# RMSNorm factors moved from GpSimd to ScalarE and VectorE, one row block cut in halves, and the first gain row spread by TensorE

## The chip, the cores and the metric

The kernel runs on one core of one Trainium2 chip. The metric is the device time of one execution in microseconds (us), the median of three runs. Five engines work side by side: TensorE (PE in the profile), VectorE (DVE), ScalarE (ACT), GpSimd (POOL) and SyncE (SP), which only issues transfers here. Each engine takes its own instructions strictly in the order in which they were written; between engines, semaphores hold an instruction back until what it reads is there.

## The reference

Four residual layers over a matrix x of 512 tokens by 1024 channels, in float32. Each layer has two sublayers, a token mixer (retention, Conformer convolution, short gated convolution, retention again) and a squared-ReLU MLP with 4096 hidden channels. Each sublayer is wrapped in two norms:

```
x <- x + RMSNorm_post( f( RMSNorm_pre(x) ) )
RMSNorm(v) = v / sqrt(mean(v*v over 1024 channels) + 1e-6) * gain
```

So between two sublayers a post-norm of the sublayer's output f, a residual add and the pre-norm of the next sublayer must be done, for all 512 tokens, and nothing of the next sublayer's product can begin before some of them are through. There are seven such places, called boundaries here, in the order of time: first (retention to MLP, layer 0), second (MLP to Conformer), third (Conformer to MLP), fourth (MLP to short convolution), fifth (short convolution to MLP), sixth (MLP to retention, layer 3), seventh (retention to MLP). The head before the first sublayer has pre-norms only, the tail after the last MLP has post-norms only.

## The kernel before, in words

Tokens are four blocks b = 0 to 3 of 128 rows (the partitions); x and f are tiles of 128 x 4 x 1024. Every float32 matrix product is made of three products of a high and a low part: the high part is a rounded copy made on ACT (`hi`, `whi`, `xin[:, 0]`), the low part the difference made on DVE (`lo`, `wlo`, `xin[:, 1]`). Weights arrive by DMA as 512 KB pieces in two buffers `raw`; line 271 (ACT) and line 282 (DVE) split them (`fetch`, `settle`), and a buffer's next load is issued by SP after its `wlo`.

A boundary is the second half of `out_final`. PE works through the last output product block by block (`block(b)`); after each block DVE or ACT adds the bank to f (`evac`), ACT squares it and sums over the row (`square`, line 415), GpSimd makes the factor (mean + 1e-6)^(-1/2) in two instructions of one column (`rstd`, lines 396 to 399), DVE multiplies f by the post gain (`fold`, line 420) and adds f times the factor to x (`add`, line 428). Then ACT sums x*x (`pre_sum`), GpSimd makes the second factor, DVE writes the normed row block into `bnd` (`pre_norm`, line 434), PE turns it (`transposes`, line 445), and `place` splits the turned block into the high and low part of `xin` (ACT line 376, DVE line 377). After block 3 PE goes on with `first_four`: eight parts of the next sublayer's first products, on the tokens of blocks 0 and 1 alone. Within it, ahead of part 3, stand the transposes of block 2, and ahead of part 7 those of block 3. The low part of `place(1)` is needed by the first part's last four products (line 340).

The order of instructions on each engine is the order of these calls in the code. In the Conformer alone a planner (`Plan`) orders the work by costs; the change does not touch it. In the head, x and the gain row arrive by DMA; the gain row (4 KB) is read 128 times by a broadcasting DMA. While nothing can be multiplied yet, `warm` runs small products.

Of the kernel before, what the change touches and what calls it, by code (L numbers as in the profile page):

```python
# [8 lines left out]
F32 = mybir.dt.float32  # L9
F32R = mybir.dt.float32r  # L10
I32 = mybir.dt.int32
AF = mybir.ActivationFunctionType
# [31 lines left out]
WARM0, WARM1 = 20, 22  # L44
# [156 lines left out]
class Trunk:  # L201
# [24 lines left out]
    def tiny(self):  # L226
        return self.cp.tile([P, 1], F32, tag="tiny", bufs=16, name=self.nm("tiny"))
# [164 lines left out]
    def rstd(self, parts):  # L392
        nc = self.nc
        ms, r = self.tiny(), self.tiny()
        if len(parts) == 2:
            nc.gpsimd.tensor_scalar(ms, parts[0], parts[1], EPS, op0=ALU.add, op1=ALU.add)  # L396
        else:
            nc.gpsimd.tensor_scalar(ms, parts[0], EPS, None, op0=ALU.add)
        nc.gpsimd.tensor_tensor(r, ms, self.neg_half, op=ALU.pow)
        return r  # L400

    def begin_boundary(self, post, pre):
# [5 lines left out]
        if pre is not None:  # L408
            nc.sync.dma_start(t[:, 1, :], self.norm_g[pre[0], pre[1]:pre[1] + 1, :].broadcast_to([P, D]))
            self.xin = self.big.tile([P, 2, 8, S], F32R, tag="xin", name=self.nm("xin"))  # L410
        self.bnd = t

    def sumsq(self, src, junk):
        acc = self.tiny()
        self.nc.scalar.activation(junk, src, AF.Square, scale=1.0 / 32.0, accum_out=acc)  # L415
        return acc
# [5 lines left out]
    def post_norm(self, b):  # L422
        self.r1[b] = self.rstd(self.sums[b])
        self.fold(b)
# [5 lines left out]
    def pre_sum(self, b):  # L430
        self.r2[b] = self.rstd([self.sumsq(self.x[:, b, :], self.bnd[:, 2 + b % 2, :])])

    def pre_norm(self, b):
        self.nc.vector.scalar_tensor_tensor(self.bnd[:, 2 + b % 2, :], self.x[:, b, :], self.r2[b],  # L434
                                            self.bnd[:, 1, :], op0=ALU.mult, op1=ALU.mult)
# [67 lines left out]
    def out_final(self, slots, mode, layer_end):  # L503
# [17 lines left out]
        def square(b, dh):  # L521
            self.sums[b].append(self.sumsq(self.f[:, b, dh * 512:(dh + 1) * 512], self.tmp()))
# [26 lines left out]

        if self.next_pre is None:  # L550
            half = slice(0, 512), slice(512, D)
            for b in range(4):
# [5 lines left out]
                else:  # L558
                    for n in range(2):
# [6 lines left out]
                        self.sums[b].append(self.sumsq(f, self.tmp()[:, :256]))  # L566
                        if n == 0:
                            t = self.tiny()
                            nc.gpsimd.tensor_tensor(t, *self.sums[b], op=ALU.add)
                            self.sums[b] = [t]  # L570
# [36 lines left out]
        post(3)  # L607
# [937 lines left out]
```

## Time and profile before

| | us |
|---|---|
| median of 3 runs (2546.22 to 2547.99) | 2546.35 |
| the profiled execution's own time | 2545.85 |
| its span, first to last instruction | 2544.1 |
| busy: PE / DVE / ACT / POOL | 2516.4 / 1652.9 / 1210.3 / 218.4 |
| mean granted TensorE clock | 0.998 |

The profile is of one execution, which lies 0.50 us under the median. Time outside the span (1.75 us) is that of starting and ending. Matmuls are pipelined and their ends are modelled, so PE at 99% says that it nearly always had work, and what can be seen best is where it waited. Busy time of an engine that nobody waits for costs nothing.

### The profile page before, as it was taken

What the parts mean: (1) busy time and instruction counts of PE and PEld (TensorE: products, weight loads), DVE (VectorE), ACT (ScalarE), POOL (GpSimd) and SP (SyncE); (2) the same over time, 40 slices, a digit from 0 to 9 for tenths busy, and PEclk for the clock granted to TensorE, in tenths of its full rate; (3) what the DMA queues carried; (4) which work ended last, traced back from release to release, by engine and by line L of the source; (5) the groups of instructions that cost most, each with busy time, mean ns of one, the idle gap of its engine ahead of it and who ended that gap; (6) DMA issues with size and microseconds to landing.
All of it is one profiled execution on the core that took longest, in us unless ns stands there. A gap on an engine that the chain in (4) does not pass through costs nothing. (4 is left out here: it accounts for less than half of the span.)

```text
span 2544.1 us, 30985 instructions
## 1 busy us (share of the span) xinstructions
PE 2516.4 (99%) x12173; PEld 2124.6 (84%) x12173; DVE 1652.9 (65%) x2151; ACT 1210.3 (48%) x1829; POOL 218.4 (9%) x248
## 2 busy tenths in 40 slices
PE   9999999999999999999999999999999999999998
PEld 8888888888888788888888888888888888888887
DVE  7665346897758977677464476784646534677773
ACT  3543444555436656544332365444344334455542
POOL 1000002000027820000010100000100000200000
PEclk9999999999999999999999999999999999999999
DMA  4323234224423532332332333314322223421331
GB/s 160 104 88 109 78 127 172 97 102 170 153 92 108 188 128 100 124 133 91 116 100 99 108 116 133 133 52 155 128 79 80 95 90 106 162 106 67 133 124 67
DMA packets 85026, 290.94 MB, mean 114 GB/s; under 512 B 9488, under 2 KB 11280, under 8 KB 84880
## 3 DMA queue, kind: packets, MB, share of 16 engines
q1 hardware_dynamic: 84880, 288.96, 32.7%
q8 instruction: 95, 1.56, 0.2%
q14 instruction: 51, 0.42, 0.0%
HBM read 265.79 MB, written 21.50 MB: 113 GB/s over the span
## 5 line engine op out<-in xcount | busy, mean ns | idle before, releaser
L337 PE MATMUL bank<-xin,whi 128*128 128x512 f32 (+1 forms) x2112 | 753.3, 365 | 2.3 <-ACT xin L376 2.3
L338 PE MATMUL bank<-xin,wlo 128*128 128x512 f32 (+1 forms) x2112 | 750.3, 364 | 0.0
L282 DVE TENSOR_TENSOR wlo<-raw,whi 128x1024 fp32r<-128x1024 f32 x340 | 416.8, 1234 | 426.5 <-ACT whi L271 425.2
L271 ACT ACTIVATE whi<-raw 128x1024 fp32r<-128x1024 f32 x340 | 354.8, 1053 | 428.9 <-DMA raw<-wall 214.7
L340 PE MATMUL bank<-xin,whi 128*128 128x512 f32 (+1 forms) x2112 | 473.8, 364 | 3.2 <-DVE xin L377 3.2
L337 PEld LDWEIGHTS bank<-xin,whi 128*128 128x128 f32 x2112 | 398.9, 189 | 65.0 <-ACT xin L376 2.9
L338 PEld LDWEIGHTS bank<-xin,wlo 128*128 128x128 f32 x2112 | 399.0, 189 | 62.2
L340 PEld LDWEIGHTS bank<-xin,whi 128*128 128x128 f32 x2112 | 369.3, 189 | 67.1 <-DVE xin L377 4.8
L266 ACT ACTIVATE whi<-blk 128x1024 fp32r<-128x1024 f32 x168 | 174.5, 1053 | 123.1 <-DVE blk L303 117.0
L280 DVE TENSOR_TENSOR wlo<-blk,whi 128x1024 fp32r<-128x1024 f32 x168 | 204.8, 1221 | 19.9 <-ACT whi L266 18.7
L396 POOL TENSOR_SCALAR tiny<-tiny,tiny 128x1 f32<-128x1 f32 x32 | 52.3, 1635 | 1484.7 <-ACT tmp L415 1483.5
L1200 ACT ACTIVATE tmp<-bank 128x512 f32<-128x512 f32 x128 | 75.2, 588 | 133.0 <-PE bank L340 133.0
L1287 DVE TENSOR_TENSOR f<-f,bank 128x512 f32<-128x512 f32 x168 | 108.4, 681 | 0.0
L1067 POOL TENSOR_TENSOR pbuf<-pbuf 128x512 f32<-128x512 f32 x69 | 100.5, 1473 | 16.0 <-ACT pbuf L1064 12.7
L327 PE MATMUL bank<-whi,hid 128*128 128x512 f32 (+1 forms) x264 | 101.5, 385 | 0.0
L329 PE MATMUL bank<-whi,hid 128*128 128x512 f32 (+1 forms) x264 | 101.0, 383 | 0.0
L328 PE MATMUL bank<-wlo,hid 128*128 128x512 f32 (+1 forms) x264 | 101.0, 383 | 0.0
L327 PE MATMUL bank<-whi,y 128*128 128x512 f32 x256 | 99.9, 390 | 0.0
L327 PE MATMUL bank<-whi,xin 128*128 128x512 f32 x256 | 99.6, 389 | 0.0
L329 PE MATMUL bank<-whi,y 128*128 128x512 f32 x256 | 99.6, 389 | 0.0
L328 PE MATMUL bank<-wlo,y 128*128 128x512 f32 x256 | 99.6, 389 | 0.0
L328 PE MATMUL bank<-wlo,xin 128*128 128x512 f32 x256 | 99.6, 389 | 0.0
(224 smaller groups left out, 4135.6 us busy)
## 6 DMA issues: line engine op xcount, KB each, us to landing
raw<-wall SPq DMA_DIRECT2D x340, 512.0 KB, 3.3
blk<-wall SPq DMA_DIRECT2D x96, 512.0 KB, 5.4
park<-x SPq DMA_DIRECT2D x20, 512.0 KB, 2.6
x<-park SPq DMA_DIRECT2D x20, 512.0 KB, 4.5
bnd<-norm_g SPq DMA_DIRECT2D x16, 512.0 KB, 6.8
phase<-tmp SPq DMA_DIRECT2D x32, 256.0 KB, 2.0
x<-x_in SPq DMA_DIRECT2D x8, 512.0 KB, 6.5
whi<-phase SPq DMA_DIRECT2D x8, 512.0 KB, 6.9
```

Of the source, the lines that this page charges most:

```text
L266: nc.scalar.activation(hi, self.form_of(c, n), AF.Copy)
L271: nc.scalar.activation(hi, self.raws[i], AF.Copy)
L280: nc.vector.tensor_sub(lo, self.form_of(c, n), hi.bitcast(F32))
L282: nc.vector.tensor_sub(lo, self.raws.pop(i), hi.bitcast(F32))
L327: nc.tensor.matmul(out, ah, bh, start=start, stop=False)
L328: nc.tensor.matmul(out, ah, bl, start=False, stop=False)
L329: nc.tensor.matmul(out, al, bh, start=False, stop=stop)
L337: self.nc.tensor.matmul(out, wh[:, c], x, start=kt == 0, stop=False)
L338: self.nc.tensor.matmul(out, wl[:, c], x, start=False, stop=False)
L340: self.nc.tensor.matmul(out, wh[:, kt * P:(kt + 1) * P], self.xin[:, 1, kt, t0:t1], start=False, stop=kt == 7)
L1067: nc.gpsimd.tensor_tensor(accs[c], accs[c], pbuf[:, slot, :], op=ALU.add)
L1287: nc.vector.tensor_add(f, f, bank)
```

## The change

Three things change. (1) `rstd`: instead of two GpSimd instructions, ACT makes a first value with its table of the reciprocal square root (`seed`), and DVE makes one Newton step on it in three instructions of one column. Where a row's sum comes in two parts, DVE first adds the first part and the 1e-6 (`more`), and the seed reads that sum. ACT thereby needs this table in the boundaries; its other tables stay as they were. (2) In a boundary, block 3 is added to x, summed and pre-normed in two halves of 512 columns. (3) In the head the first gain row is loaded once, into one partition, and spread to 128 by two products with a row of ones; the loads of x and of the first weights alternate; `warm` runs 6 and 8 products instead of 20.

```diff
-WARM0, WARM1 = 20, 22
+WARM0, WARM1 = (6, 8), 22
...
             self.nc.vector.tensor_sub(lo, val, hi.bitcast(F32))
-    def rstd(self, parts):
+    def sumsq(self, src, junk):
+        acc = self.tiny()
+        self.nc.scalar.activation(junk, src, AF.Square, scale=1.0 / 32.0, accum_out=acc)
+        return acc
+    def more(self, sums, src, junk):
         nc = self.nc
-        ms, r = self.tiny(), self.tiny()
-        if len(parts) == 2:
-            nc.gpsimd.tensor_scalar(ms, parts[0], parts[1], EPS, op0=ALU.add, op1=ALU.add)
+        acc = self.sumsq(src, junk)
+        if not sums:
+            sums.append(self.eps)
         else:
-            nc.gpsimd.tensor_scalar(ms, parts[0], EPS, None, op0=ALU.add)
-        nc.gpsimd.tensor_tensor(r, ms, self.neg_half, op=ALU.pow)
+            base = self.tiny()
+            nc.vector.tensor_scalar(base, sums[1], sums[0], None, op0=ALU.add)
+            sums[:] = [base]
+        sums.append(acc)
+    def seed(self, sums):
+        r0 = self.tiny()
+        self.nc.scalar.activation(r0, sums[1], AF.Abs_reciprocal_sqrt, bias=sums[0])
+        sums.append(r0)
+    def rstd(self, sums):
+        nc = self.nc
+        base, acc, r0 = sums
+        t, r = self.tiny(), self.tiny()
+        nc.vector.tensor_scalar(t, acc, base, r0, op0=ALU.add, op1=ALU.mult)
+        nc.vector.tensor_scalar(t, t, r0, -0.5, op0=ALU.mult, op1=ALU.mult)
+        nc.vector.tensor_scalar(r, t, 1.5, r0, op0=ALU.add, op1=ALU.mult)
         return r
     def begin_boundary(self, post, pre):
...
         if post is not None:
             nc.sync.dma_start(t[:, 0, :], self.norm_g[post[0], post[1]:post[1] + 1, :].broadcast_to([P, D]))
         if pre is not None:
-            nc.sync.dma_start(t[:, 1, :], self.norm_g[pre[0], pre[1]:pre[1] + 1, :].broadcast_to([P, D]))
+            self.gain = t[:, 1, :]
+            nc.sync.dma_start(self.gain, self.norm_g[pre[0], pre[1]:pre[1] + 1, :].broadcast_to([P, D]))
             self.xin = self.big.tile([P, 2, 8, S], F32R, tag="xin", name=self.nm("xin"))
         self.bnd = t
-    def sumsq(self, src, junk):
-        acc = self.tiny()
-        self.nc.scalar.activation(junk, src, AF.Square, scale=1.0 / 32.0, accum_out=acc)
-        return acc
     def fold(self, b, cols=slice(0, D)):
         f = self.f[:, b, cols]
         self.nc.vector.tensor_mul(f, f, self.bnd[:, 0, cols])
     def post_norm(self, b):
+        self.fold(b)
         self.r1[b] = self.rstd(self.sums[b])
-        self.fold(b)
     def add(self, b, cols=slice(0, D)):
         x = self.x[:, b, cols]
         self.nc.vector.scalar_tensor_tensor(x, self.f[:, b, cols], self.r1[b], x, op0=ALU.mult, op1=ALU.add)
-    def pre_sum(self, b):
-        self.r2[b] = self.rstd([self.sumsq(self.x[:, b, :], self.bnd[:, 2 + b % 2, :])])
-    def pre_norm(self, b):
-        self.nc.vector.scalar_tensor_tensor(self.bnd[:, 2 + b % 2, :], self.x[:, b, :], self.r2[b],
-                                            self.bnd[:, 1, :], op0=ALU.mult, op1=ALU.mult)
+    def pre_sum(self, b, parts=(slice(0, D),)):
+        self.sums2[b] = []
+        for c in parts:
+            self.more(self.sums2[b], self.x[:, b, c], self.bnd[:, 2 + b % 2, c])
+        self.seed(self.sums2[b])
+    def pre_norm(self, b, parts=(slice(0, D),)):
+        r = self.rstd(self.sums2.pop(b))
+        for c in parts:
+            self.nc.vector.scalar_tensor_tensor(self.bnd[:, 2 + b % 2, c], self.x[:, b, c], r,
+                                                self.gain[:, c], op0=ALU.mult, op1=ALU.mult)
     def transposes(self, b):
         nc = self.nc
...
-            self.sums[b].append(self.sumsq(self.f[:, b, dh * 512:(dh + 1) * 512], self.tmp()))
+            self.more(self.sums[b], self.f[:, b, dh * 512:(dh + 1) * 512], self.tmp())
+            if dh:
+                self.seed(self.sums[b])
 
...
-                        self.sums[b].append(self.sumsq(f, self.tmp()[:, :256]))
-                        if n == 0:
-                            t = self.tiny()
-                            nc.gpsimd.tensor_tensor(t, *self.sums[b], op=ALU.add)
-                            self.sums[b] = [t]
+                        self.more(self.sums[b], f, self.tmp()[:, :256])
...
-        post(3)
+        self.post_norm(3)
+        for c in half:
+            self.add(3, c)
+        if layer_end:
...
-                self.pre_sum(3)
-                self.pre_norm(3)
+                self.pre_sum(3, half)
+                self.pre_norm(3, half)
...
-            self.ln_eps = self.const(LN_EPS, "ln_eps")
+            self.ln_eps, self.eps = self.const(LN_EPS, "ln_eps"), self.const(EPS, "eps")
+            self.table(AF.Abs_reciprocal_sqrt)
-            self.r1, self.r2, self.turned = {}, {}, {}
+            self.r1, self.sums2, self.turned = {}, {}, {}
-            for b in range(2):
-                nc.sync.dma_start(self.x[:, b, :], self.x_in[b])
-            self.begin_boundary(None, (LAYERS[0], 0))
-            self.load()
-            self.load()
-            for b in range(2, 4):
+            self.begin_boundary(None, None)
+            self.xin = big.tile([P, 2, 8, S], F32R, tag="xin", name="xin0")
+            row, self.gain, one = self.bnd[0:1, 0, :], self.bnd[:, 1, :], self.tmp(P)[0:1, :]
+            nc.vector.memset(one, 1.0)
+            nc.sync.dma_start(row, self.norm_g[LAYERS[0], 0:1, :])
+            for b in range(4):
...
-                self.r2[b] = self.rstd([self.sumsq(self.x[:, b, :], self.f[:, b, :])])
+                self.sums2[b] = []
+                self.more(self.sums2[b], self.x[:, b, :], self.f[:, b, :])
+                self.seed(self.sums2[b])
...
-            self.warm(WARM0)
+            self.warm(WARM0[0])
+            for n in range(2):
+                bank, c = self.bank(), slice(512 * n, 512 * n + 512)
+                nc.tensor.matmul(bank, one, row[:, c], start=True, stop=True)
+                nc.vector.tensor_copy(self.gain[:, c], bank)
+            self.warm(WARM0[1])
```

Of 64 factors, 32 post and 32 pre, each now has three DVE instructions and one ACT instruction of one column in place of two of GpSimd; where there are two parts, one more DVE instruction stands ahead. The program has four more ACT table loads: one ahead of the first seed of the first, the third and the seventh boundary, one in the last retention.

DVE in the fourth boundary, from the post-norm of block 3 to its pre-norm, before (`wlo` is the weight split, `xin` the placing of block 2, L434 the pre-norm):

```order
L420 TENSOR_TENSOR f_8227<-f_8227,bnd_10031 128x1024
L428 SCALAR_TENSOR_TENSOR x_9768<-f_8227,tiny_10365,x_9768 128x1024
L282 TENSOR_TENSOR wlo_10376<-raw_10133,whi_10375 128x1024
L282 TENSOR_TENSOR wlo_10432<-raw_10163,whi_10431 128x1024
L377 TENSOR_TENSOR xin_10034<-bank_10421,xin_10034 128x4x128
L377 TENSOR_TENSOR xin_10034<-bank_10426,xin_10034 128x4x128
L434 SCALAR_TENSOR_TENSOR bnd_10031<-x_9768,tiny_10444,bnd_10031 128x1024
```

and now, at the same place (L406 is the sum of the first part, L420 to L422 the Newton step, L458 the pre-norm):

```order
L420 TENSOR_SCALAR tiny_10524<-tiny_10511,tiny_10513,tiny_10515 128x1
L421 TENSOR_SCALAR tiny_10524<-tiny_10524,tiny_10515 128x1
L422 TENSOR_SCALAR tiny_10525<-tiny_10524,tiny_10515 128x1
L447 SCALAR_TENSOR_TENSOR x_9899<-f_8358,tiny_10525,x_9899 128x512 x2
L282 TENSOR_TENSOR wlo_10537<-raw_10264,whi_10536 128x1024
L282 TENSOR_TENSOR wlo_10593<-raw_10294,whi_10592 128x1024
L377 TENSOR_TENSOR xin_10165<-bank_10582,xin_10165 128x4x128
L377 TENSOR_TENSOR xin_10165<-bank_10587,xin_10165 128x4x128
L406 TENSOR_SCALAR tiny_10606<-tiny_10602,eps 128x1
L420 TENSOR_SCALAR tiny_10610<-tiny_10604,tiny_10606,tiny_10608 128x1
L421 TENSOR_SCALAR tiny_10610<-tiny_10610,tiny_10608 128x1
L422 TENSOR_SCALAR tiny_10611<-tiny_10610,tiny_10608 128x1
```

Three small instructions stand ahead of the add, which is now two halves, and four ahead of the pre-norm; the first of these four makes the operand of the seed, and it stands behind the weight splits and the placing of block 2.

SP at the start of the program, before (`early` is the first weight tiles):

```order
L1387 DMA x_91<-x_in 128x1024 x2
L409 DMA bnd_95<-norm_g 128x1024
L252 DMA early<-wall 128x1024 x2
L1392 DMA x_91<-x_in 128x1024
L252 DMA early<-wall 128x1024
```

and now:

```order
L1418 DMA bnd_95<-norm_g 1x1024
L1420 DMA x_93<-x_in 128x1024
L252 DMA early<-wall 128x1024
L1420 DMA x_93<-x_in 128x1024
L252 DMA early<-wall 128x1024
```

The broadcast of the gain (128 rows) is gone, its one row stands first, and the second block of x stands behind the first weight tile.

## Rows read from the trace of the kernel before

**Rows 1.** Waits of PE in the whole span: line, whom for, us, times, longest.
```profile
PE bank L445 <- DVE bnd L434: 8.2, 8, 2.5
...
PE bank L340 <- DVE xin L377: 3.2, 8, 0.9
PE bank L337 <- ACT xin L376: 2.3, 2, 2.0
```

**Rows 2.** Timeline of DVE, fourth boundary: start, us, instruction, idle before and its releaser.
```profile
1273.15 1.28 DVE L434 SCALAR_TENSOR_TENSOR bnd<-x,tiny,bnd 128x1024 f32<-128x1024 f32 x1 [1.58 <-POOL tiny L399]
...
1275.55 1.22 DVE L420 TENSOR_TENSOR f<-f,bnd 128x1024 f32<-128x1024 f32 x1
1276.87 1.28 DVE L428 SCALAR_TENSOR_TENSOR x<-f,tiny,x 128x1024 f32<-128x1024 f32 x1
...
1279.27 0.68 DVE L515 TENSOR_TENSOR f<-f,bank 128x512 f32<-128x512 f32 x1
1280.33 1.29 DVE L434 SCALAR_TENSOR_TENSOR bnd<-x,tiny,bnd 128x1024 f32<-128x1024 f32 x1 [0.39 <-POOL tiny L399]
1281.54 1.22 DVE L420 TENSOR_TENSOR f<-f,bnd 128x1024 f32<-128x1024 f32 x1
1283.52 1.29 DVE L428 SCALAR_TENSOR_TENSOR x<-f,tiny,x 128x1024 f32<-128x1024 f32 x1 [0.76 <-POOL tiny L399]
...
1286.99 1.28 DVE L377 TENSOR_TENSOR xin<-bank,xin 128x512 fp32r<-128x512 f32 x2
1288.19 1.28 DVE L434 SCALAR_TENSOR_TENSOR bnd<-x,tiny,bnd 128x1024 f32<-128x1024 f32 x1
```

**Rows 3.** Timeline of PE, fourth boundary.
```profile
1278.81 0.74 PE L340 MATMUL bank<-xin,whi 128*128 128x256 f32 x4 [0.30 <-DVE xin L377]
...
1289.61 1.06 PE L445 MATMUL bank<-ident,bnd 128*128 128x128 f32 x8 [0.56 <-DVE bnd L434]
```

**Rows 4.** Timeline of DVE in the rotary set-up, one after another.
```profile
27.32 0.49 DVE L1306 TENSOR_SCALAR tmp<-tmp,small 128x512 f32<-128x512 f32 x1
27.84 0.43 DVE L1310 TENSOR_SCALAR tmp<-tmp 128x512 f32<-128x512 f32 x1
```

**Rows 5.** Groups of DVE: busy us, mean ns of one, idle before.
```profile
L843 DVE TENSOR_TENSOR mask<-ident 128x64 f32<-128x64 f32 x1 | 0.2, 219 | 0.0
...
L1364 DVE MEMSET neg_half<- 128x1 f32 x1 | 0.1, 59 | 0.8 <-PEq L1537 0.8
```

**Rows 6.** Instructions of line 231 on ACT: ns min/median/max, first and last start.
```profile
L231 ACT ACT_TABLE_LOAD  x2: 1283/1283/1283, 874.7 to 890.4; - x2
L231 ACT ACTIVATE tiny<-ln_eps x2: 203/204/206, 876.0 to 891.6; 128x1 f32<-128x1 f32 x2
```

**Rows 7.** Groups of ACT: busy us, mean ns, idle before.
```profile
L1114 ACT ACTIVATE tmp<-tmp,ln_eps 128x512 f32<-128x512 f32 x1 | 0.7, 722 | 1.1 <-DVE tmp L1111 1.1
...
L1117 ACT ACTIVATE tmp<-tmp 128x512 f32<-128x512 f32 x1 | 0.6, 630 | 0.0
```

**Rows 8.** Timeline of ACT, second boundary.
```profile
758.02 0.31 ACT L882 ACTIVATE shift<-ones 128x128 fp32r<-128x128 f32 x1 [4.21 <-DVE ones L881]
```

**Rows 9.** Timeline of ACT, sixth boundary.
```profile
1811.76 1.06 ACT L271 ACTIVATE whi<-raw 128x1024 fp32r<-128x1024 f32 x1 [6.95 <-DMA raw<-wall]
```

**Rows 10.** Timeline of DVE in the head.
```profile
8.67 2.48 DVE L434 SCALAR_TENSOR_TENSOR bnd<-x,tiny,bnd 128x1024 f32<-128x1024 f32 x2 [7.76 <-DMA bnd<-norm_g]
...
17.63 1.28 DVE L434 SCALAR_TENSOR_TENSOR bnd<-x,tiny,bnd 128x1024 f32<-128x1024 f32 x1 [0.46 <-POOL tiny L399]
...
21.57 1.27 DVE L434 SCALAR_TENSOR_TENSOR bnd<-x,tiny,bnd 128x1024 f32<-128x1024 f32 x1
```

**Rows 11.** Transfers from 0 to 22 us, rate in 40 equal slices.
```profile
GB/s 0 0 0 238 261 268 395 425 335 253 238 216 268 343 417 380 447 402 432 402 447 410 425 417 417 415 381 370 380 350 387 421 406 391 253 145 56 0 0 0
```

**Rows 12.** Timeline of DVE in the tail.
```profile
2539.58 1.41 DVE L428 SCALAR_TENSOR_TENSOR x<-f,tiny,x 128x512 f32<-128x512 f32 x2 [0.84 <-POOL tiny L399]
```

**Rows 13.** Windows: stretch, us, busy us of each engine, granted clock, DMA, GB/s.
```profile
1813.00:1817.00 4.00, 3.64 (x22) 3.65 (x23) 3.41 (x4) 1.74 (x3) 0.00 (x0) 0.72 0.40 131
```

More of the change, by code (lines that the diff above doesn't have):

```diff
@@ L226, in tiny @@
     def tiny(self):
-        return self.cp.tile([P, 1], F32, tag="tiny", bufs=16, name=self.nm("tiny"))
+        return self.cp.tile([P, 1], F32, tag="tiny", bufs=26, name=self.nm("tiny"))
     def table(self, func):
@@ L548, in post @@
                 layer_end(b)
+        half = slice(0, 512), slice(512, D)
         if self.next_pre is None:
-            half = slice(0, 512), slice(512, D)
             for b in range(4):
@@ L565, in out_final @@
                         nc.vector.tensor_add(f, f, bank[:, c])
-                        self.sums[b].append(self.sumsq(f, self.tmp()[:, :256]))
-                        if n == 0:
-                            t = self.tiny()
-                            nc.gpsimd.tensor_tensor(t, *self.sums[b], op=ALU.add)
-                            self.sums[b] = [t]
+                        self.more(self.sums[b], f, self.tmp()[:, :256])
+                    self.seed(self.sums[b])
                 self.r1[b] = self.rstd(self.sums[b])
@@ L606, in out_final @@
         self.pre_norm(2)
-        post(3)
+        self.post_norm(3)
+        for c in half:
+            self.add(3, c)
+        if layer_end:
+            layer_end(3)
         def start(i):
@@ L1377, in build @@
             self.angles = [dram.tile([P, S], F32, name=f"angle{n}") for n in range(2)]
-            self.neg_half = self.const(-0.5, "neg_half")
             self.half_pi = self.const(float(np.float32(math.pi / 2)), "half_pi")
-            self.ln_eps = self.const(LN_EPS, "ln_eps")
+            self.ln_eps, self.eps = self.const(LN_EPS, "ln_eps"), self.const(EPS, "eps")
+            self.table(AF.Abs_reciprocal_sqrt)
             self.ident = cp.tile([P, P], F32, name="ident")
```

## The prediction

> **What bounds the kernel now.** I read the page's busy times first: PE has work nearly throughout, so only its waits can be won, and whatever makes a wait longer is paid in full. The view of PE's waits then says where they lie: it waits for the pre-norm on VectorE ahead of transposes, for the low parts of the placed blocks on VectorE, and a little for the high parts on ScalarE [rows 1]. That is 8.2 + 3.2 + 2.3 = 13.7 us over the head and seven boundaries, the most that any better boundary could return. Third, the timelines of one ordinary boundary, the fourth: the reader is to see that VectorE works from 1273.15 to the pre-norm of block 3 at 1288.19 almost without a hole; its two holes, 0.39 and 0.76 us, end on GpSimd [rows 2]. PE waits for VectorE twice there, 0.30 us for the low part of block 1 and 0.56 us for the pre-norm of block 3 [rows 3]. So VectorE's own queue, not GpSimd's delay alone, sets the end of a boundary.
>
> **The price of the new small instructions.** None of the kinds on one column is in the trace of before, so I bound it. VectorE's two-input instruction takes 219 ns on 64 columns [rows 5] and 0.68 us on 512 [rows 2]: 1.03 ns a column, and 0.15 us left at one column. A scalar read from memory adds 0.49 - 0.43 = 0.06, and an instruction that needs the one before it starts 0.03 after its end (27.32 + 0.49 to 27.84) [rows 4]. So a step of a dependent chain is 0.24 us, and a factor's three are 0.72. From below: the one-column memset takes 59 ns [rows 5]; with the wait, 0.09 a step, 0.27 for three. From above: a second scalar in the first step and 0.02 more of waiting at each, 0.85. I take 0.72, since 64 columns is the nearest row that reads its inputs. ScalarE's one-column instruction takes 0.204 [rows 6]; a bias from memory adds 722 - 630 = 92 ns [rows 7]; the seed is 0.30, 0.33 with its wait, between 0.2 and 0.4. An independent small sum costs VectorE 0.14, since neighbours overlap.
>
> On the fixed part the Trainium skill, "VectorE: DVE Perf Modes", section "The TRN2 errata", has two statements: a table by which VectorE from SBUF to SBUF needs 58 cycles plus the columns, an estimated 61 ns at one column, and beside it that the measured fixed term is about 150 cycles. The 219 ns at 64 columns speak for the second; by the first three steps would be about 0.3, and the time the one of the first rival.
>
> **One ordinary boundary, step by step.** Up to the pre-norm of block 1 the new steps come out nearly even: a factor waited 0.39 to 1.58 us for GpSimd [rows 2], now it waits for a seed and three steps; I take the shift there as -0.15. From then on VectorE is full, and what is added counts:
> - fold of block 2 to its add: 1.32 us before (1275.55 to 1276.87); now 1.14 to the next free issue, then 0.72: 1.86, so +0.54. The placing of block 1 and PE's low products come that much later.
> - drain of block 3 to pre-norm of block 2: 1.06 before (1279.27 to 1280.33); now 0.60 + 0.14 + 0.72 = 1.46, so +0.40.
> - fold to add of block 3: 1.98 before (1281.54 to 1283.52), GpSimd ending it; now 1.86, so -0.12.
> - the add in halves: two of 0.75 hold the queue for 1.34 instead of 1.20, so +0.14.
> - the weight splits and the placing of block 2 are unchanged, but then the pre-norm of block 3 followed at once (1286.99 to 1288.19), its factor having come from GpSimd meanwhile. Now the first small sum stands behind the placing, ScalarE's seed waits for that sum, and the three steps wait for the seed: 0.24 + 0.33 + 0.72 = 1.29, all uncovered.
> - the pre-norm in halves lets the first four transposes start after 0.75 instead of 1.28; PE ends them all at 2.00 after its start instead of 2.29: -0.29.
> The sum is -0.15 + 0.54 + 0.40 - 0.12 + 0.14 + 1.29 - 0.29 = +1.8 us, some 0.4 of it at the low products and the rest at the last transposes. Queued behind the waiting steps are weight splits; they come 0.8 us later, which PE does not feel, as the pieces that it reads by then are already split. Nothing behind the boundary gives the time back, for PE has no other holes.
>
> **The other boundaries.** The first, third and seventh have the same order plus a table load ahead of the first seed. A load takes 1.28 us and the next instruction starts as it ends (874.7 to 876.0) [rows 6]. Part of it hides in the wait for block 1's product; by the same steps 0.45 stays, so 2.25 each. In the fifth ScalarE drains the banks itself, and each seed delays a drain: 1.9. In the second ScalarE cannot go on before a memset that stands on VectorE behind the adds [rows 8], so its later sums move with them; 1.5. In the sixth PE ends by waiting for ScalarE, which waits 6.95 us for a weight transfer [rows 9]; the transfer is issued on SP behind the parking of block 3, so only the shift of the adds, 0.8, is paid, and the later transposes hide in that wait. Together 1.8 + 3 x 2.25 + 1.9 + 1.5 + 0.8 = 12.75. One more table load, in the last retention, stands where ScalarE waits for products: nothing; uncovered, 1.3.
>
> On such loads the Trainium skill, "ScalarE: Activation LUTs", section "What ACT_TABLE_LOAD costs", reckons a drain of 1.38 us behind the load, 2.66 in all. The starts of line 231, 1.3 us apart, show none; by the page the sum would be up to 3 x 1.4 = 4 us more.
>
> **Head and tail.** Before, the first two pre-norms waited until 8.67 for the broadcast gain [rows 10]. That wait goes: the row is there early, and two products and two copies spread it before ScalarE has block 0's sum. But block 1 of x now stands behind a 512 KB weight tile, at 400 GB/s [rows 11] 1.3 us; with its sum, seed and three steps its pre-norm starts at about 9.8, where the second of the pair started before (8.67 + 1.24 = 9.9). The first products therefore start as they did. Behind them the factors for blocks 2 and 3, until now made beside VectorE's work, stand in it: the pre-norm of block 2 goes from 17.63 to 18.1 (the second weight split waits 0.3 for two more seeds; then three steps instead of a hole of 0.46), that of block 3 from 21.57 to 22.8, and PE meets both: +1.2. In the tail the hole of 0.84 ahead of the last adds [rows 12] is refilled by seed, three steps and a fold that stood beside GpSimd before: 0, between -0.3 and +0.3.
>
> **Sum.** 12.75 + 1.2 = 13.95. On the profiled execution's 2545.85 that gives 2559.8; it lies 0.5 under the median of the runs, so 2560.
>
> **Rivals.**
> 1. Small steps are cheap, and it gets faster. Place: every three steps in the boundaries. With 0.27 for three, VectorE reaches the add of block 2 early, PE's wait for the low part goes, and transposes begin nearly on arrival: by the steps above about -0.85 in five boundaries, -1.0 in the second, -1.6 in the sixth, nothing in the head, -6.9 in all: 2539. It decides from about 0.46 for three down, where an ordinary boundary comes out even. For it: the 59 ns row. Against: every row of VectorE that reads operands, and GpSimd's holes on VectorE add to only 1.15 us in the late stretch.
> 2. Three steps near 0.46 (0.12 + 0.03 each): boundaries +0.1 to +0.4, sixth -0.6, head +0.4: 2547, no change.
> 3. The longer waits lower TensorE's clock. After two waits in the sixth boundary the granted clock averages 0.72 from 1813 to 1817 [rows 13], part of it at 1.2 GHz, which loses 4 x 0.28 = 1.1 us. If the head (fewer warming products, more holes) and all the other boundaries go that way, 7 x 1.1 = 7.7 more: 2568. Against: the longest single wait of line 445, 2.5 us [rows 1], is followed by no such stretch.
>
> **Numbers.** Forecast 58%, with its own range of 2551 to 2565; first rival 14%, second 17%, third 11%. The range for 8 in 10 reaches to 2545 below, leaving out most of the first rival, and 2570 above. About 0.2%, 5 us, is what a measurement here can tell from no change: faster 0.14, same 0.20, slower 0.66.
>
> **What would show it.** In the changed kernel's profile: small steps of lines 420 to 422 near 0.21 us each; VectorE without GpSimd holes but as late; PE's wait for the low part about 0.8 instead of 0.3 and its wait for the last transposes about 1.9 in an ordinary boundary; the pre-norm of block 1 in the head near 9.8. Small steps of 0.1 us would make the forecast wrong at its root; a head that starts 2 us earlier, or a lower clock, would be wrong in size only.

## The result and the profile after

The changed kernel takes 2567.88 us (median, 2567.65 to 2569.79); the kernel before took 2547.17 beside it (2546.22 to 2548.65). The ratio is 1.0089 with a 95% interval of 1.0076 to 1.0101: slower by 20.7 us. The forecast was 2560 with a range of 2545 to 2570; the direction and the main mechanism came as forecast, the loss was half as large again, and the time lies outside the forecast's own range of 2551 to 2565. The profiled execution took 2567.91, its span is 2566.1 (2544.1 before), the mean granted clock 0.996 (0.998).

Where the time went is read best at one place that each boundary has: the start of the first product of `first_four`. In the two profiled executions these starts stand apart as follows (each column is what a stretch adds; the last one runs to PE's last product). The sum is that of these two executions, 22.0 us; between the medians it is 20.7.

| us | head | 1st | 2nd | 3rd | 4th | 5th | 6th | 7th | sum |
|---|---|---|---|---|---|---|---|---|---|
| after minus before | 3.03 | 3.71 | 4.08 | 2.75 | 2.48 | 3.48 | -0.09 | 2.60 | 22.04 |
| forecast | 1.2 | 2.25 | 1.5 | 2.25 | 1.8 | 1.9 | 0.8 | 2.25 | 13.95 |

The tail is as it was: from the start of PE's last product to the end of the span 7.42 before and 7.41 after.

PE's waits after (line, whom for, us, times, longest) answer to [rows 1]; line 469 is the transposes there:

```profile
PE bank L469 <- DVE bnd L458: 16.9, 10, 3.0
PE bank L340 <- DVE xin L377: 9.6, 8, 1.5
...
PE bank L337 <- ACT xin L376: 0.2, 1, 0.2
```

Both waits for VectorE have grown, 8.2 to 16.9 and 3.2 to 9.6. Of the 2.3 for ScalarE the 2.0 in the sixth boundary are gone: PE's waits for VectorE ahead of it grew there from 1.3 to 3.5, so PE comes to it later. The groups of the new small instructions on VectorE (instructions, busy us, mean ns, idle before):

```profile
L422 DVE TENSOR_SCALAR tiny<-tiny,tiny 128x1 f32<-128x1 f32 x64 | 13.7, 214 | 2.2
L421 DVE TENSOR_SCALAR tiny<-tiny,tiny 128x1 f32<-128x1 f32 x64 | 13.7, 214 | 2.3
L420 DVE TENSOR_SCALAR tiny<-tiny,tiny,tiny 128x1 f32<-128x1 f32 x39 | 10.6, 271 | 7.9 <-ACT tiny L412 7.9
L406 DVE TENSOR_SCALAR tiny<-tiny,eps 128x1 f32<-128x1 f32 x39 | 8.1, 207 | 0.0
```

They last 207 to 271 ns, about as much as the 219 ns for the 64 columns of [rows 5] and three and a half to four and a half times the memset there. VectorE's timeline of the fourth boundary answers to [rows 2]:

```profile
1278.50 0.69 DVE L539 TENSOR_TENSOR f<-f,bank 128x512 f32<-128x512 f32 x1 [0.73 <-PE bank L329]
...
1286.10 0.27 DVE L420 TENSOR_SCALAR tiny<-tiny,eps,tiny 128x1 f32<-128x1 f32 x1 [0.82 <-ACT tiny L412]
...
1286.90 1.29 DVE L458 SCALAR_TENSOR_TENSOR bnd<-x,tiny,bnd 128x1024 f32<-128x1024 f32 x1
...
1289.30 1.22 DVE L439 TENSOR_TENSOR f<-f,bnd 128x1024 f32<-128x1024 f32 x1
1290.44 0.27 DVE L420 TENSOR_SCALAR tiny<-tiny,tiny,tiny 128x1 f32<-128x1 f32 x1
1290.74 0.22 DVE L421 TENSOR_SCALAR tiny<-tiny,tiny 128x1 f32<-128x1 f32 x1
1290.99 0.21 DVE L422 TENSOR_SCALAR tiny<-tiny,tiny 128x1 f32<-128x1 f32 x1
1291.24 1.28 DVE L447 SCALAR_TENSOR_TENSOR x<-f,tiny,x 128x1024 f32<-128x1024 f32 x1
...
1293.64 0.68 DVE L539 TENSOR_TENSOR f<-f,bank 128x512 f32<-128x512 f32 x1
...
1295.16 1.28 DVE L458 SCALAR_TENSOR_TENSOR bnd<-x,tiny,bnd 128x1024 f32<-128x1024 f32 x1
1296.36 1.22 DVE L439 TENSOR_TENSOR f<-f,bnd 128x1024 f32<-128x1024 f32 x1
...
1298.30 1.41 DVE L447 SCALAR_TENSOR_TENSOR x<-f,tiny,x 128x512 f32<-128x512 f32 x2
...
1301.90 1.28 DVE L377 TENSOR_TENSOR xin<-bank,xin 128x512 fp32r<-128x512 f32 x2
1303.10 0.20 DVE L406 TENSOR_SCALAR tiny<-tiny,eps 128x1 f32<-128x1 f32 x1
1303.73 0.27 DVE L420 TENSOR_SCALAR tiny<-tiny,tiny,tiny 128x1 f32<-128x1 f32 x1 [0.42 <-ACT tiny L412]
...
1304.53 1.42 DVE L458 SCALAR_TENSOR_TENSOR bnd<-x,tiny,bnd 128x512 f32<-128x512 f32 x2
```

The three steps stand between the fold of block 2 (1289.30) and its add (1291.24), with VectorE never idle: 1290.44 to 1291.24 is 0.80. At the end a chain that nothing covers: small sum at 1303.10, seed, three steps, pre-norm at 1304.53. On PE this becomes the two waits that answer to [rows 3], 1.10 instead of 0.30 and 2.02 instead of 0.56 (the expectations below count from start to start, beyond the usual spacing of the products, and call the same two waits 1.26 and 2.18):

```profile
1293.18 0.74 PE L340 MATMUL bank<-xin,whi 128*128 128x256 f32 x4 [1.10 <-DVE xin L377]
...
1305.43 1.23 PE L469 MATMUL bank<-ident,bnd 128*128 128x128 f32 x8 [2.02 <-DVE bnd L458]
```

Behind three of these waits TensorE's clock falls to its lower level, 1.2 GHz. The view by windows (stretch, us, busy us of PE, PEld, DVE, ACT, POOL, granted clock, DMA share, GB/s), behind the first, second and fifth boundary:

```profile
431.00:434.00 3.00, 3.00 (x16) 3.00 (x16) 2.86 (x4) 1.58 (x3) 0.00 (x0) 0.50 0.47 173
773.00:778.00 5.00, 4.78 (x23) 4.81 (x24) 4.48 (x6) 2.15 (x3) 0.00 (x0) 0.50 0.40 139
...
1489.00:1492.00 3.00, 3.00 (x15) 3.00 (x15) 2.69 (x4) 2.06 (x3) 0.00 (x0) 0.50 0.35 106
```

Before, these stretches ran at 1.00. Behind the sixth boundary [rows 13], in the Conformer and in the tail the clock fell before, and it falls there after as well. The third, fourth and seventh boundary have as long a wait after (2.0) and keep the full clock.

The head, on VectorE, answers to [rows 10]:

```profile
8.01 0.69 DVE L1451 COPY bnd<-bank 128x512 f32<-128x512 f32 x1 [1.01 <-PE bank L1450]
...
9.42 1.29 DVE L458 SCALAR_TENSOR_TENSOR bnd<-x,tiny,bnd 128x1024 f32<-128x1024 f32 x1
...
11.42 1.29 DVE L458 SCALAR_TENSOR_TENSOR bnd<-x,tiny,bnd 128x1024 f32<-128x1024 f32 x1
...
19.79 1.28 DVE L458 SCALAR_TENSOR_TENSOR bnd<-x,tiny,bnd 128x1024 f32<-128x1024 f32 x1
...
24.52 1.28 DVE L458 SCALAR_TENSOR_TENSOR bnd<-x,tiny,bnd 128x1024 f32<-128x1024 f32 x1
```

The pre-norms of blocks 0, 2 and 3, which started at 8.67, 17.63 and 21.57, start at 9.42, 19.79 and 24.52. That of block 1 stood right behind that of block 0 and began 1.2 after it; now its three steps stand between the two, and it begins at 11.42. What holds the first is no longer a transfer but the two copies of the gain, and these wait for the products that spread it, on PE:

```profile
4.20 3.78 PE L1450 MATMUL bank<-bnd,tmp 1*128 1x512 f32 x4
7.91 3.48 PE L237 MATMUL bank<-ident 128*128 128x128 f32 x16
```

The second line is the 8 warming products behind them, two records each. They start 0.21 us apart almost to their end and 0.11 apart from 10.9 on; before the change the spacing went from 0.21 to 0.11 at 5.7. So TensorE worked at half pace in the head until then. The column of the granted clock says 1.00 there, but the trace has no record of the clock ahead of these two moments (10.9 after, 5.7 before), and the spacing is what can be trusted.

### The profile page after: what moved, and what is told of

Same layout as the page of the kernel before. It is cut to its first block, busy times and chain, and to the rows that moved or that the text cites. A ratio compares the mean times of both kernels' runs of the same rounds, so it can differ in the third digit from the quotient of the medians.

```text
span 2566.1 us, 31121 instructions
## 1 busy us (share of the span) xinstructions
PE 2524.7 (98%) x12165; PEld 2129.0 (83%) x12165; DVE 1703.1 (66%) x2400; ACT 1236.8 (48%) x1912; POOL 114.8 (4%) x119
## 4 chain that ended last, share of the span: by engine, by line
PE 86%; DVE 8%; POOL 3%; ACT 2%; issue 1%; DMA 0%; DVEq 0%; POOLq 0%; SPq 0%; ACTq 0%
PE bank L337 15%; PE bank L338 15%; PE bank L340 15%; PE bank L329 13%; PE bank L327 13%; PE bank L328 13%; POOL pbuf L1094 2%; DVE bnd L458 1%; DVE x L447 1%; DVE f L439 1%; DVE xin L377 1%; DVE wlo L282 1%; ACT bnd L394 1%; DVE tiny L420 1%; DVE tiny L421 1%
## 5 line engine op out<-in xcount | busy, mean ns | idle before, releaser
L327 PE MATMUL bank<-whi,xin 128*128 128x512 f32 x256 | 99.6, 389 | 0.0
L329 PE MATMUL bank<-whi,xin 128*128 128x512 f32 x256 | 99.6, 389 | 0.0
```

What stands on the lines that cost most here:

```text
L327: nc.tensor.matmul(out, ah, bh, start=start, stop=False)
L329: nc.tensor.matmul(out, al, bh, start=False, stop=stop)
```

## The experiments

The theory under test: the three small steps, on VectorE's queue where it has no hole, carry the loss, and the longer waits of PE pull the clock down behind some boundaries. The rivals: the halving of block 3 with its seed that waits for a small sum; ScalarE's seeds and table loads; the head. All runs are given against the kernel before, which ran beside them (2545.8 to 2546.0 us). The changed kernel did not run again beside them: differences from it are taken from its 2567.88, beside which the kernel before took 2547.17, so they are uncertain by 1 to 2 us.

**The head of before put back.** Edit: `begin_boundary(None, (LAYERS[0], 0))`, the old order of loads and `warm(20)`.

> The changed kernel with the head of before: gain row by the broadcasting load, loads of x and warming products as before; the factors are still made by a seed on ScalarE and three steps on VectorE. Theory (serial small steps in the boundaries carry most of the loss): block 3's pre-norm in the head returns from 24.5 us to about 22.8, not to 21.6, since its three steps stay; 2568 - 1.7 = 2566. Rival 1 (the head's spread products are the cause): near 2548. Rival 2 (the new head gains what the forecast supposed, the loss lies wholly elsewhere): 2568 or slower.

Measured 2568.77 (2565.73 to 2570.22), ratio 1.0089 [1.0075, 1.0102]. By its time the head costs nothing. Its trace says more: the pre-norm of block 3 in the head stands at 23.02 (22.8 expected), `first_four` of the first boundary comes 1.52 behind that of before where the changed kernel comes 3.03 behind. So 1.5 of the head is the new head and 1.5 the small steps; in the time, 1.5 us don't show in a spread of 4.5. The clock's falls came behind other boundaries than in the changed kernel (the first, third, fifth and sixth). The rival by which the head carries the loss fell.

**GpSimd's factors in the changed kernel.**

```diff
...
-        self.nc.scalar.activation(r0, sums[1], AF.Abs_reciprocal_sqrt, bias=sums[0])
...
+        nc.gpsimd.tensor_scalar(ms, sums[0], EPS, None, op0=ALU.add)
+        nc.gpsimd.tensor_tensor(r, ms, self.neg_half, op=ALU.pow)
...
```

`rstd` returns this value without VectorE's steps, and the sum of two parts stands on GpSimd too.

> The changed kernel with every factor made by GpSimd's two instructions again (for two-part sums the add of the parts stands on GpSimd too); halves of block 3 and the new head stay, no table of the reciprocal square root is loaded. Theory (the steps on VectorE are the cause): the boundaries return to those of before, or 0.15 each better by the earlier transposes, the new half-speed stretches of TensorE go; the head keeps part of its 2.9: 2547 + 2 - 1 = 2548, between 2545 and 2551. Rival 1 (halving block 3 is the cause): about 1.3 us a boundary stay, 2557 or more. Rival 2 (the head is the cause): 2565.

Measured 2546.76, ratio 1.0002 [0.9993, 1.0010]: the whole loss is gone with the way the factor is made, halves and new head being there still. In this run's head TensorE came to full pace at 4.3, and its clock fell again behind PE's wait of 2.5 us for the second pre-norm (the changed kernel, at half pace until 10.9, has no such fall):

```profile
8.00:12.00 4.00, 1.34 (x11) 0.91 (x9) 1.72 (x3) 3.07 (x5) 0.79 (x2) 0.89 1.03 419
12.00:16.00 4.00, 4.00 (x18) 3.77 (x19) 3.89 (x6) 2.64 (x4) 0.00 (x0) 0.50 0.91 314
```

**No Newton step.**

```diff
     def rstd(self, sums):
...
+        return sums[2]
```

> The changed kernel without the Newton step: the factor is ScalarE's table value itself (this leaves out the Newton step, so the factors are less accurate). Seeds, table loads, small sums, halves and head stay. Theory (three dependent steps of 0.81 us, four times on VectorE's path in a boundary): an ordinary boundary loses its wait for the low part (1.26 to about 0.4) and most of that for the last transposes (2.18 to 0.2 to 0.6), about 2.5 us in five boundaries, 1.5 in two, 1.6 in the head, and the half-speed stretches that came go (5): 2568 - 22 = 2546, between 2540 and 2550. Rival 1 (seed's wait for the small sum, table loads and halving are the cause): 4 us gained, 2564. Rival 2 (the lower clock is a thing of its own): 2551.

Measured 2530.62 (2529.55 to 2531.51), ratio 0.9937 [0.9925, 0.9950]: not 22 us less than the changed kernel but 37, and 15 less than the kernel before: a miss (2540 to 2550 was expected), the theory's way but larger. The expectation kept waits of 0.2 to 0.6 that in fact vanished: the fourth boundary came 3.8 us shorter than in the changed kernel, where 2.5 had been reckoned, and the sixth 5.1, where at most 2.5 had. The tail became 1.0 shorter. PE's waits in it (the transposes are line 463 there):

```profile
PE bank L463 <- DVE bnd L452: 0.4, 2, 0.2
PE bank L337 <- ACT xin L376: 0.4, 2, 0.2
```

In its fourth boundary the add of block 2 follows its fold after 1.25 (1.32 before, 1.94 after), and the pre-norm of block 2 stands 0.72 behind the drain (1.06 before, 1.52 after):

```profile
1269.80 1.22 DVE L433 TENSOR_TENSOR f<-f,bnd 128x1024 f32<-128x1024 f32 x1
1271.05 1.28 DVE L441 SCALAR_TENSOR_TENSOR x<-f,tiny,x 128x1024 f32<-128x1024 f32 x1
...
1273.55 0.68 DVE L533 TENSOR_TENSOR f<-f,bank 128x512 f32<-128x512 f32 x1
1274.14 0.21 DVE L406 TENSOR_SCALAR tiny<-tiny,eps 128x1 f32<-128x1 f32 x1
1274.27 1.28 DVE L452 SCALAR_TENSOR_TENSOR bnd<-x,tiny,bnd 128x1024 f32<-128x1024 f32 x1
```

Seeds, table loads, halves and the new head are all in this kernel; so none of them carries the loss by itself.

**Block 3 whole.** `self.add(3)`, `self.pre_sum(3)` and `self.pre_norm(3)` without `half`.

> The changed kernel with block 3 of a boundary whole again (add, sum and pre-norm in one piece, so no small sum between the placing of block 2 and the seed); Newton steps and head stay. Theory: the seed is made beside the weight splits and the placing of block 2, so the small sum of 0.24 and the wait of 0.42 for the seed go, the add holds the queue 0.14 less, the last transposes start 0.29 later: about -0.5 in each of seven boundaries, -3.5 in all, and one or two half-speed stretches of 1.7 us may go with it: 2568 - 4.5 = 2563. Rival 1 (halving is the main cause): 2553 or less. Rival 2 (halving pays): 2570 or more.

Measured 2562.51, ratio 1.0062 [1.0049, 1.0074]; 2563 was expected. With the steps there, halving costs 5 us by the medians (6.4 between the profiled executions). How, its intervals say: against the changed kernel the third, fourth, sixth and seventh boundary gain 0.39 to 0.41 each, but the first 1.85, the second 1.32 and the fifth 1.95. In the first and fifth the stretch at the lower clock is gone (3.4 us each by the clock's records), which prices it at 1.5 us; in the second it is half as long. It is gone in the sixth too, and there that gains nothing, for PE now waits 1.0 for ScalarE instead. PE in its fourth boundary:

```profile
1289.61 0.74 PE L340 MATMUL bank<-xin,whi 128*128 128x256 f32 x4 [1.10 <-DVE xin L377]
...
1301.63 1.06 PE L469 MATMUL bank<-ident,bnd 128*128 128x128 f32 x8 [1.79 <-DVE bnd L458]
```

The wait of 2.02 became 1.79 and the transposes 1.06 instead of 1.23; that gave back 0.4 where the clock had stayed up, and 1.9 where a fall went with it.

**Two Newton steps.** The three lines of `rstd` stand twice.

> The changed kernel with two Newton steps on every factor instead of one (six dependent one-column instructions on VectorE). A dose: the runs so far gave 2531 without any step and 2568 with one. Theory (every step that is added stands in full on VectorE's path, 0.81 us a factor): from the fold of block 2 on four factors, 3.2 us more in an ordinary boundary, 7 x 3.2 = 22, 1.6 in the head, and up to two half-speed stretches (3.4): 2593, between 2588 and 2600, with PE's two waits of the fourth boundary going from 1.26 and 2.18 to about 2.1 and 4.6. Rival (the cost of one step was a threshold, for instance the clock falling once a wait passes some length, and not the work on VectorE): 2575 or less.

Measured 2621.91, ratio 1.0303 [1.0289, 1.0317]: 54 us more, twice what was expected, a miss. Its waits:

```profile
PE bank L472 <- DVE bnd L461: 55.2, 25, 3.8
PE bank L340 <- DVE xin L377: 4.6, 6, 1.0
```

59.8 instead of 26.5: 33 us more. The expectation had counted the four factors from block 2 on alone; but the holes ahead of them were used up by the first step already, so now PE waits for the first transposes too (25 waits instead of 10). Of the other 21 us the tail has 2.1. The rest goes, by estimate, to the clock: behind or within every boundary it falls twice (54.6 us of records in the boundaries, 17.1 in the changed kernel; half of the difference is 19), and once in the head. No run parts waits and clock here.

**Table value, block 3 whole, head of before** (the edits of the first, third and fourth run together).

> ScalarE's table value as the factor (the Newton step is left out, so the factors are less accurate), block 3 of a boundary whole, the head of before. The run without the Newton step, with halves and the new head, took 2530.6. Theory: the small sum and the wait for it go (0.4), the transposes of block 3 start 0.29 later, the head gives 1 back: 2529, between 2526 and 2532. Rival (halving by itself pays once no serial small steps stand ahead of the pre-norm): 2533 or more.

Measured 2530.01 (2529.18 to 2530.90), ratio 0.9942 [0.9930, 0.9955]. As expected, and level with 2530.62.

**Seeds that nobody reads, in the kernel before** (besides the two lines: the constant 1e-6, a first load of the table, and 26 instead of 16 one-column buffers).

```diff
...
+        r0 = self.tiny()
+        nc.scalar.activation(r0, parts[-1], AF.Abs_reciprocal_sqrt, bias=self.eps)
         return r
```

> The kernel before, with ScalarE making a reciprocal square root of every sum besides, which nobody reads: the factors come from GpSimd as before. It prices the seeds (0.3 us each) and the four table loads (1.28 each) on ScalarE alone. Theory (VectorE's steps are the cause): ScalarE has room but for the start of the three boundaries with a load, at most 0.45 each, and the fifth: +0 to +2, 2546 to 2548. Rival (table loads and ScalarE's queue carry a good part of the loss): 2552 or more.

Measured 2545.32, ratio 1.0000 [0.9991, 1.0009]. The seeds and the table loads, as work on ScalarE's queue, cost nothing that can be measured. What VectorE's waiting for a seed costs is not in this run, since nobody reads them.

**Halves alone, in the kernel before** (written as the changed kernel with GpSimd's factors and the head of before).

> The kernel before with only block 3 of a boundary in halves (add, sum and pre-norm), factors by GpSimd and the head of before. The run with the halves, GpSimd's factors and the new head took 2546.8, its first boundary came 2.3 us later than before's, with a half-speed stretch of 6.8 us in the head. Theory: halving by itself gains, since PE's last transposes start as the first half is written: about 0.35 a boundary, 2.5 in all, and the head is that of before: 2543.5, between 2541 and 2545.5. Rival 1 (halving gains nothing): 2546. Rival 2 (halving costs): 2549.

Measured 2545.59, ratio 1.0000 [0.9991, 1.0009]: halving by itself is neither gain nor loss; the 2.5 us expected did not come. In an ordinary boundary the wait for the transposes does shrink (0.56 to 0.15):

```profile
1280.05 0.74 PE L340 MATMUL bank<-xin,whi 128*128 128x256 f32 x4 [0.25 <-DVE xin L377]
...
1290.45 1.23 PE L463 MATMUL bank<-ident,bnd 128*128 128x128 f32 x8 [0.15 <-DVE bnd L452]
```

but the intervals show only 0.2 for it there: the transposes run into the second half (1.23 instead of 1.06), and in the seventh PE then waits 0.3 for the high part. One fall of the clock went (sixth) and one came (second).

**16 small products ahead of the transposes of block 3.**

```diff
...
+            for _ in range(fill if m == 0 else 0):
+                nc.tensor.matmul(bk[:, 0, :], self.ident, self.ident, start=True, stop=True)
```

> The changed kernel with 16 small products of the identity (109 ns each, 1.74 us) on PE ahead of the transposes of block 3 in every boundary, written into the bank that the first transpose then overwrites. They lie in PE's wait of 1.9 to 3.1 us for the pre-norm, which stays as long by the end of VectorE's work. Theory: the half-speed stretches behind the boundaries (17.0 us of records in the profiled execution of the changed kernel, 430.8, 772.1, 1488.9 and 1830.2) come from PE standing idle, go with it, and had cost half their length: 2568 - 8.5 = 2559.5, between 2557 and 2563. Rival 1 (these stretches cost nothing, for what they lose is hidden in later waits, or they have another cause than the wait): 2566 to 2569. Rival 2 (the small products delay the transposes): over 2570.

Measured 2569.00, ratio 1.0090 [1.0076, 1.0104]: no gain where 2559.5 was expected (2557 to 2563), a miss, and still it tells something. Each such float32 product appears twice, so that 16 take 3.57 us, not 1.74, and outlast the wait:

```profile
1303.10 3.73 PE L468 MATMUL bank<-ident 128*128 128x128 f32 x32
1306.67 1.04 PE L471 MATMUL bank<-ident,bnd 128*128 128x128 f32 x8
```

The clock now stays up where it had fallen:

```profile
430.00:434.00 4.00, 4.00 (x38) 4.00 (x37) 2.98 (x5) 2.27 (x4) 0.00 (x0) 1.00 0.33 116
...
1489.00:1493.00 4.00, 4.00 (x38) 4.00 (x37) 2.71 (x5) 1.57 (x4) 0.00 (x0) 1.00 0.30 111
```

Against the changed kernel the third, fourth and seventh boundary lose 1.21 to 1.23 by the filling, while the first and fifth come out at +0.01 and -0.07: there a fall of the clock is repaid, again 1.2 to 1.3 us each. The second, which had the longest stretch, comes out at -2.15 and the sixth at -0.46. With the wait filled no boundary has a fall: so the falls come from PE's idling, and they cost time. Another 0.76 is lost in the head, which the filling does not touch: there TensorE came to full pace only at 14.0. A filling of half the length was not tried.

**The Newton step on blocks 0 and 1 only, and on blocks 2 and 3 only.** `if not (b in (0, 1)): return r0`, and the same with `(2, 3)`; both leave out the tail's steps too.

> The changed kernel with the Newton step on the factors of blocks 0 and 1 only; those of blocks 2 and 3, and of the tail, are ScalarE's table values (their Newton step is left out). With no Newton step at all it took 2530.6, with all 2567.9. Theory (place decides: up to the pre-norm of block 1 VectorE has holes while it waits for PE, from the fold of block 2 on it has none): from evac of block 1 to fold of block 2 it takes 10.8 us as in the changed kernel, which GpSimd's factors needed too (10.6); then no steps follow. PE waits about 0.4 for the low part, nothing for the transposes; 7 x 0.4 and 0.8 in the head: 2534.5, between 2532 and 2538. Rival (each step costs alike wherever it stands): half of 37, 2549.

> The changed kernel with the Newton step on the factors of blocks 2 and 3 only; those of blocks 0, 1 and of the tail are ScalarE's table values (their Newton step is left out). Theory (place decides): VectorE comes to the fold of block 2 1.86 us earlier than in the changed kernel (8.94 instead of 10.80 behind the evac of block 1), PE's wait for the low part (1.26) goes, that for the last transposes is 2.18 - 1.86 + 1.26 = 1.6: 7 x 1.6 = 11, 1 in the head, one half-speed stretch (1.7): 2544.5, between 2541 and 2548, so much dearer than the steps of blocks 0 and 1. Rival (each step costs alike): 2549; then this run and that with the steps of blocks 0 and 1 alone take the same time.

Measured 2540.57, ratio 0.9978 [0.9969, 0.9987], and 2548.78, ratio 1.0012 [1.0003, 1.0022]. Against no step at all that is 10 and 18 us. Place does decide, but less than expected (4 and 14): both times lie above their ranges (2538 and 2548), and the second is the rival's 2549, while the first is not. First the fourth boundary with the steps of blocks 0 and 1, then that with those of blocks 2 and 3, on PE:

```profile
1279.27 0.74 PE L340 MATMUL bank<-xin,whi 128*128 128x256 f32 x4 [0.42 <-DVE xin L377]
```

```profile
1294.13 1.23 PE L471 MATMUL bank<-ident,bnd 128*128 128x128 f32 x8 [1.51 <-DVE bnd L460]
```

The waits are as computed (0.4, and 1.5 for 1.6). What the first sum lacked are the boundaries with a table load and the fifth, where PE waits about 0.4 more, the second, where it waits 1.3 for the transposes of block 3, and the sixth, which lay 2.4 above the one without steps and has a wait of 1.2 for ScalarE; the second sum lacked above all the sixth, 3.4 above. Together the two make 28, the whole step 37. The 9 between are of three kinds: PE waits 26.5 for VectorE in the changed kernel, but 6.2 and 14.3 in these two; it ran 20.5 us at the lower clock there, but 3.4 and 10.2 here (3.4 without any step); and 1.0 is the tail. So each half finds some of the holes that the other fills, and fewer falls of the clock come with it; how the 9 split was not measured.

**Table value, halves, head of before.**

> ScalarE's table value as the factor (the Newton step is left out), block 3 of a boundary in halves, the head of before. It stands between the run with halves and the new head (2530.6) and that with the whole block 3 and the head of before (2530.0). Theory: halves and whole are even, since neither leaves PE a wait of note in a boundary, and the two heads are even within 1: 2530, between 2528.5 and 2531.5. Rival (halves gain 2 to 3 us, which the new head had hidden): 2527.5.

Measured 2530.60 (2530.05 to 2530.75), ratio 0.9938 [0.9926, 0.9951], as expected. The head of before brings PE to the first boundary 2.4 us earlier than the new one, and the time is the same; two waits take most of it back (1.0 in the first stretch, 0.8 in the sixth):

```profile
PE bank L337 <- ACT xin L376: 1.2, 2, 0.9
PE bank L329 <- DVE own L377: 0.7, 1, 0.7
```

The longest of the first line, 0.9, stands in the sixth boundary, in front of ScalarE's split of a weight that comes by a transfer [rows 9], the second ahead of the first MLP; neither is in the profile of the run with the new head.

## Why the prediction was right in direction and short in size

**What bounds the kernel.** Right. VectorE's queue sets the end of a boundary; a step more in it is a wait more on PE. The dose of 0, 1 and 2 steps gives 2530.6, 2567.9 and 2621.9; GpSimd's factors, the rest unchanged, give 2546.8.

**The price of the small steps.** Right within its bounds: 0.81 for three (starts 0.31, 0.25 and 0.25 apart) where 0.72 was taken and 0.85 was the upper bound; the seed 0.295 (0.30), the small sum 0.12 (0.14). The first rival needed 0.46 or less. On the two statements of the Trainium skill, "VectorE: DVE Perf Modes", section "The TRN2 errata": the 207 ns at one column here lie above both, and nearer to the fixed term of about 150 cycles than to the 61 ns estimated from the table.

**The ordinary boundary.** Step by step, forecast and measured in the fourth: up to the fold of block 2, -0.15 and +0.18 (10.80 behind the drain of block 1, 10.62 before); fold to add of block 2, 0.54 and 0.62; drain of block 3 to pre-norm of block 2, 0.40 and 0.46; fold to add of block 3, -0.12 and -0.04; halves of the add, 0.14 and 0.13; small sum, seed and three steps, 1.29 and 1.43; earlier transposes, -0.29 and -0.35 (from the pre-norm's start to their end the rows of before give 2.48 where 2.29 was reckoned; only the difference entered). The sum is 2.43 for 1.8, and the interval 2.48. No step of the path was missing. The first had the wrong sign (0.33 off); the next largest difference is the uncovered chain at the end (0.14).

**The other boundaries.** Waits of PE alone (spacing of its products beyond the usual) grew by 2.66, 1.80, 2.58, 2.25, 1.78, 0.20 and 2.66, 13.9 for the 12.75 forecast. The 0.8 of the sixth did not come: what PE waited more for VectorE it no longer waited for ScalarE. The table loads cost 0.4 (0.45 forecast), and none is followed by a drain: ScalarE's load at 398.41 ends at 399.69 and the seed starts at 399.70, as in [rows 6].

**The clock.** Here the forecast was short: it had it as a rival only, at 11%. By the records 20.5 us ran at the lower level (10.2 before, the tail apart and the start of the head, which has no record); half of the difference, 5.1 us, is the estimate of its cost, with the 1.2 to 1.5 measured for a stretch beside it. The rival's own price, 1.1, came from a window that ended before the stretch did: at half pace the 3.4 us of the record would lose 1.7. The rival was wrong in that all boundaries would go: it was the first, second and fifth. The head did, in its way: in the profiled executions TensorE stayed at half pace there until 10.9 instead of 5.7. Its argument against itself, the 2.5 us wait that no fall had followed, holds: the length of the wait alone does not decide, for 2.0 us were followed by a fall in the first boundary and by none in the third, fourth and seventh. What does stays open.

**The head.** The failed step: "The first products therefore start as they did." They start at 14.11 instead of 12.55. The spread of the gain was put at nothing because it would be done before ScalarE had block 0's sum; its products took 3.78 us, at TensorE's half pace, the second copy ended at 8.70, and block 0's factor, whose steps stand behind that copy, was ready at 9.4. Block 1's steps and pre-norm stand behind block 0's, so it started at 11.42 and not at 9.8. This gives 1.5; the small steps of the head gave 1.5 for the 1.2 forecast. With the head of before put back the first products start at 12.61.

**Tail.** Right: nothing.

**The sum.** 13.9 + 3.0 + 5.1 = 22.0, as the intervals have it; the first two are measured, the last is an estimate. The measured time is that of the third rival, 2568, but not by its sum: that is luck. The time also lies outside the forecast's own range and inside the wide one by 2 us.

The three fastest kernels here, at 2530 to 2531, leave out the Newton step and take the table's value as the factor; how exact that has to be is for the user of the kernel to say, not for the trace.

## What to carry to other kernels

On a full queue count instructions, not columns: a chain of three one-column instructions cost VectorE 0.81 us, more than half of a pass over 1024 columns, and replacing a hole by such a chain gains only where the hole was longer. The cost grew faster than the number of steps here, 37 us for the first step and 54 for the second: where the queue still had holes the steps fell into them in part, then they stood in full, and behind more of the longer waits TensorE's clock fell. Before a factor is refined on a critical engine, price the version without the refinement: here it was the difference between 15 us gained and 21 lost.

## What had not been expected of the hardware

- The two products that spread the gain took 3.78 us in the changed kernel and 2.00 us in the run with GpSimd's factors, both written alike and started at 4.20. The pace of TensorE differed, not the products: the warming products behind them took 3.48 us in the changed kernel, as shown with the result, and here 2.05. The granted clock reads 1.00 in both; in the changed kernel only because its trace has no clock record there.

```profile
4.20 2.00 PE L1444 MATMUL bank<-bnd,tmp 1*128 1x512 f32 x4
6.14 2.05 PE L237 MATMUL bank<-ident 128*128 128x128 f32 x16
```

- By the spacing of its products TensorE came to full pace between 5.2 and 7.5 us in every profiled run with the head of before. With the new head, whose warming is interrupted by the spread, it came at 4.3 and 4.5 in two runs and between 10.9 and 14.1 in six. What decides between the two stays open.
- A float32 product of 128 x 128 by the identity shows as two records 109 ns apart; 16 of them took 3.57 us.
- A fall of the clock after a wait of PE came in some boundaries and not in others with the same wait, and moved when other parts of the kernel were changed.
